# An encoder block on one NeuronCore: memory values copied out of PSUM while their scale is unknown, the first operand in one transfer, eleven unit products at the front

## The chip, the cores and the metric

The kernel runs on one core of one Trainium2 chip. The metric is the device time of one execution in microseconds (us). Before the change the median of three runs is 1365.81 us (1365.35 to 1368.44).

## The reference

One layer of a bidirectional encoder on 256 tokens of width 2048, with 256 memory tokens. All data is float32.

```python
h = rms_norm(x, g_mix);  proj = h @ w_in        # q/k/v of mixers A and B, q of C, three gates
mkv = rms_norm(mem, g_mem[layer]) @ w_mem_kv[layer]
kc = rms_norm(split_heads(mkv[..., :C_W], C_HEADS), g_kc[layer])
vc = split_heads(mkv[..., C_W:], C_HEADS)
...
x = x + merged @ w_o[layer]
hf = rms_norm(x, g_ffn[layer]) @ w_ffn_in[layer]
x = x + (jax.nn.silu(hf[..., :D_FF]) * hf[..., D_FF:]) @ w_ffn_out[layer]
```

Mixer A is a dilated window attention with a relative bias, B a grouped-query attention with rotary embedding, C a cross-attention of four heads into the memory. Their outputs are multiplied by sigmoid gates, merged and projected. For this change two things matter: the memory's normalised rows are projected to four key heads (kc) and four value heads (vc), and a row's normalisation is a single factor per token, so that it can be applied after the projection.

## The kernel before

**Products.** Every float32 operand is split in two parts (`split`, L129): ScalarE writes the rounded high part (whi, or the high half of memT, xT, V: L132 without a scale, L135 with one), VectorE the remainder (wlo: L133, L136). A product of two operands is then three matmuls: high by high, high by low, low by high. All matmuls are issued through one helper line, L79. Weights come in blocks of 512 KB (two k-tiles of 128 rows by 512 columns), loaded by SP into seven raw buffers (`load`, L216), and split into four buffers of whi and four of wlo. A block gives 12 matmuls of 128x512.

**The first stages.** `beginning` (L807) projects the memory through `pair` with two column blocks at once: c = 0 gives the four kc heads in the banks mmY and mmX (tag "at"), c = 1 the four vc heads in mmW and mmQ (tag "tp"; there are two banks of that tag). In this stage the splits of `pair` stand in line 438 (`halves`, whi) and line 448 (`low`, wlo). Then eight calls of `product` (L232) multiply x by w_qkv, one block of 512 columns each; they take their two banks by turns from the tags "c1" and "tp" (made = 1 takes "c1", made = 2 "tp"). Each result goes to `take_slots` (L657) as a job beside the products.

**take_slots.** For heads other than values it copies the bank to SBUF at once, on ScalarE: the squares to sq (L667), the values to y (L668); VectorE sums the squares (L669). Value heads stay in their banks until the rows' scale is known: a job yields as long as its name is not in `known` (L672), and then V is split from the bank, scaled by the row factor (L679, through `split`, L135 and L136), one head and one half of the tokens at a time. The row factor comes from `row_sums` (L288): four row blocks are loaded into SBUF, squared and summed by ScalarE (L296), and a Newton iteration on VectorE (`root_of`, L138) gives the factor. It runs beside the memory projection for the memory ("mem"), and beside the first product for x. Key and query heads are then scaled (L691), multiplied by their gain on GpSimd (L712) and transposed by TensorE (hT).

**Slots.** The tiles rows, y, sq, oneh, row and others are allocated by `s4` and share five slots of 4 KB per partition (pool mid, L111).

**What sets the order.** Inside `run` (the memory projection, and everything from the merging on) TensorE's and SP's instructions keep the program's order. In the products over w_qkv and the attention beside them, the order on each engine is computed from priorities and simulated times when the kernel is built; jobs advance by one step at each k-tile (`tick`, L189), and what stands in a high_priority block goes first. Each engine then executes its instructions in that order.

**The first microseconds.** After the identity matrix is there, TensorE runs unit products on it (L349 to L351). The first operand block (memT, k = 0 and 1) is loaded in two halves of 128 KB with the two halves of the first weight block between them: `whole` (L499) calls `operand(0, True, 1)`, then `load` with two parts, and `load` calls `between` ahead of its second part.

Of the kernel before, what the change touches and what calls it, by code (L numbers as in the profile page):

```python
# [14 lines left out]
AF = mybir.ActivationFunctionType  # L15
# [3 lines left out]
P = 128  # L19
S = 256  # L20
T = S // P
D = 2048
KT = D // P
HD = 128
# [3 lines left out]
PK = 2  # L28
# [75 lines left out]
def encoder_block(ctx: ExitStack, tc: tile.TileContext, a: dict, out: bass.AP):  # L104
    nc = InOrder(tc)
# [16 lines left out]
    def s4(shape, name, dt=F32):  # L122
        return mid.tile(shape, dt, name=name, tag="s4")
# [89 lines left out]

        free.append(place_of.pop(id(raw))[1])

    def load(src, k0, nk, parts=1, between=None):  # L216

        place = free.pop(0)
        raw = place[0].tile([P, PK, NC], F32, name=place[1], bufs=1)
        place_of[id(raw)] = raw, place  # L220
        c = k0 % PK * NC
        for k in range(0, nk, nk // parts):
            n = nk // parts
            if k and between:
                between(k0 + k)
            nc.sync.dma_start(out=raw[:, k:k + n].rearrange("p k n -> p (k n)"),
                              in_=src[k0 // PK][:, c + k * NC:c + (k + n) * NC])
        return raw
# [32 lines left out]
    def load_T(src, g, tag):  # L261


        tiles = [s8([P, 4, 2, S], tag) for _ in range(KT // 4)]
        raws, fetched, have = {}, set(), set()

        def get(k, fetch=False, n=2):
            k0 = k // 2 * 2
            tl = tiles[k // 4]
            ks = range(k0, k0 + 2) if n == 2 else (k,)  # L270
            if k0 not in raws:
                raws[k0] = early.tile([P, 2, S], F32, name="rawT", bufs=4)
            if not fetched.intersection(ks):
                nc.sync.dma_start(out=raws[k0][:, ks[0] - k0:ks[0] - k0 + n],
                                  in_=src[k0 // 2].rearrange("p (k s) -> p k s", s=S)[:, ks[0] - k0:ks[0] - k0 + n])
            fetched.update(ks)
            if not fetch:
                for i in ks:
                    if i not in have:
                        have.add(i)  # L280
                        split(tl[:, i % 4, 0], tl[:, i % 4, 1], raws[k0][:, i - k0], g[:, i:i + 1])
            return tl[:, k % 4, 0], tl[:, k % 4, 1]
        get.tiles = tiles
        return get

    known = set()
# [60 lines left out]
    make_identity(tc.nc, ident)  # L347

    idle = bank("idle", "tp")  # L349
    for _ in range(8):  # L350
        nc.tensor.matmul(idle[:, :P], lhsT=ident, rhs=ident, start=True, stop=True)  # L351

    two = const.tile([P, 2], F32, name="two")
# [96 lines left out]
    def pair(src, lhs, lists, done, doubles=(), forms=None, operand=None, fresh="", early=False, by_halves=False):  # L450
# [48 lines left out]
        def whole(u, c):  # L499
            def ready():  # L500
                last_kind[0] = ""
                parts = 2 if operand and u + c == 0 else 1
                if operand and c == 0:
                    operand(2 * u, True, 3 - parts)
                raw = load((src(u, c),), 0, PK, parts, lambda k: operand(k, True, 1))
                if parts == 2:
                    pass
                elif operand and c == 0:
                    operand(2 * u)
                elif operand and 2 * u + 2 < KT:  # L510
                    operand(2 * u + 2, True)
                hi, lo = halves(*(raw[:, k] for k in range(PK)) if parts == 2 else (raw,),
                                each=(lambda k: operand(k, False, 1)) if parts == 2 else None)
                release(raw)

                def products():
                    halved = by_halves and c == 0 and left[ends[0][1]] == 2
                    for i in range(2 * T):
                        t, k = (i % T, i // T) if parts == 2 else (i // 2, i % 2)
                        st = at(2 * u + k, t)  # L520
                        if not (halved and t):
                            mul(ends[c][t], st, hi[:, k], lo[:, k], parts == 2)
                    for i in range(4 * halved):
                        st, k = at(2 * u + i % 2, 1), i % 2
                        mul(ends[0][1], st, hi[:, k], lo[:, k], cols=slice(i // 2 * NC // 2, (i // 2 + 1) * NC // 2))
                    ending()
                return products
            return ready
# [128 lines left out]
    def take_slots(ps, slots, r, name="x"):  # L657

        n = sum(s[0][0] != "v" for s in slots)
        if n:  # L660
            y = s4([P, T, 4, HD], "y")
            sq = s4([P, T, 4, HD], "sq")
            ss = small.tile([P, T, 4], F32, name="hss")
            with tc.high_priority():
                for t in range(T):
                    src = ps[t][:, :n * HD].rearrange("p (n d) -> p n d", d=HD)
                    nc.scalar.activation(sq[:, t, :n], src, AF.Square)  # L667
                    nc.scalar.activation(y[:, t, :n], src, AF.Copy)  # L668
                nc.vector.tensor_reduce(ss[:, :, :n], sq[:, :, :n], axis=AX.X, op=ALU.add)  # L669
        if name not in known:  # L670
            yield EVAC_LAG
        while name not in known:  # L672
            yield None
        with tc.high_priority():
            for i in range(n, len(slots)):
                v = s2.tile([P, 2, T, HD], F32R, name="V", tag="s2")
                V[slots[i]] = v
                for t in range(T):
                    split(v[:, 0, t], v[:, 1, t], ps[t][:, i * HD:(i + 1) * HD], r[:, 0, t:t + 1])  # L679
        if n:  # L680
            yield EVAC_LAG
            v = small.tile([P, T, 4], F32, name="hv")
            f = small.tile([P, T, 4], F32, name="hf")
            each = lambda w: r[:, w].unsqueeze(2).broadcast_to([P, T, n])
            nc.vector.tensor_mul(ss[:, :, :n], ss[:, :, :n], each(1))
            nc.vector.tensor_scalar(v[:, :, :n], ss[:, :, :n], 1.0 / HD, EPS, op0=ALU.mult, op1=ALU.add)
            nc.vector.tensor_mul(f[:, :, :n], rsqrt(v[:, :, :n], [P, T, n]), each(0))
            yield EVAC_LAG
            for t in range(T):
                for j in range(n):  # L690
                    nc.scalar.activation(y[:, t, j], y[:, t, j], AF.Copy, scale=f[:, t, j:j + 1])  # L691
            turned = slots[0][0][1] == "b"
            rot = s4([P, T, 4, HD], "rot") if turned else None
            j = 0
            while j < n:
                m = 1
                while j + m < n and slots[j + m][0] == slots[j][0]:
                    m += 1
                if turned:
                    tab = turns[:, ("qb", "kb").index(slots[j][0])]  # L700
                    for t in range(T):
                        cs, sn = (tab[:, w, t].unsqueeze(1).broadcast_to([P, m, HD]) for w in range(2))
                        yt, other = y[:, t, j:j + m], sq[:, t, j:j + m]
                        nc.vector.tensor_mul(rot[:, t, j:j + m], yt, cs)
                        pairs = lambda v: v.rearrange("p n (d c) -> p n d c", c=2)
                        for c in range(2):
                            nc.vector.tensor_mul(pairs(other)[:, :, :, c], pairs(yt)[:, :, :, 1 - c],
                                                 pairs(sn)[:, :, :, c])
                        nc.vector.tensor_add(rot[:, t, j:j + m], rot[:, t, j:j + m], other)
                else:  # L710
                    g = gh[:, HEAD_GAINS.index(slots[j][0])]
                    nc.gpsimd.tensor_mul(y[:, :, j:j + m], y[:, :, j:j + m],  # L712
                                         g.unsqueeze(1).unsqueeze(1).broadcast_to([P, T, m, HD]))
                j += m
            y = rot if turned else y
        if n:
            yield HEAD_LAG
            for j in range(n):
                tp = bank("hT")
                for t in range(T):  # L720
                    nc.tensor.transpose(tp[:, t * P:(t + 1) * P], y[:, t, j], ident)
                hT = s2.tile([P, 2, S], F32R, name="headT", tag="s2")
                with tc.high_priority():
                    split(hT[:, 0], hT[:, 1], tp[:, :S])
                headT[slots[j]] = hT
                if j % 2 and j < n - 1:
                    yield 1
        yield 2
        run_jobs()
# [374 lines left out]
```

## Time and profile before

| | |
|---|---|
| median of 3 runs | 1365.81 us |
| lowest, highest | 1365.35, 1368.44 us |
| profiled execution | 1366.78 us, its span 1365.0 us |
| granted TensorE clock, mean of the span | 0.997 |
| TensorE, VectorE, ScalarE busy | 99%, 85%, 63% |
| read from HBM | 297.17 MB, 220 GB/s over the span |

The span runs from the first to the last instruction of the profiled execution. A row of the timeline gives the start in us from the start of the span, the duration, the engine, the line, the operation, what it writes and reads, and how many instructions were merged into it; in brackets stand the engine's idle time before it and what ended it. A row of busy time in a stretch gives for the stretch its length and the busy time of TensorE's matmuls (PE), its weight loads (PEld), VectorE (DVE), ScalarE (ACT) and GpSimd (POOL), each with its number of instructions, then the granted TensorE clock as a share of full speed, the DMA engines' busy share and GB/s. SPq rows are DMA issues of SyncE.

### The profile page before, as it was taken

What the parts mean: (1) busy time and instruction counts of PE and PEld (TensorE: products, weight loads), DVE (VectorE), ACT (ScalarE), POOL (GpSimd) and SP (SyncE); (2) the same over time, 40 slices, a digit from 0 to 9 for tenths busy, and PEclk for the clock granted to TensorE, in tenths of its full rate; (3) what the DMA queues carried; (4) which work ended last, traced back from release to release, by engine and by line L of the source; (5) the groups of instructions that cost most, each with busy time, mean ns of one, the idle gap of its engine ahead of it and who ended that gap; (6) DMA issues with size and microseconds to landing.
All of it is one profiled execution on the core that took longest, in us unless ns stands there. A gap on an engine that the chain in (4) does not pass through costs nothing.

```text
span 1365.0 us, 17319 instructions
## 1 busy us (share of the span) xinstructions
PE 1354.4 (99%) x6170; PEld 1122.6 (82%) x6170; DVE 1157.6 (85%) x1412; ACT 855.6 (63%) x1110; POOL 53.1 (4%) x60
## 2 busy tenths in 40 slices
PE   9989999999999999999999999999999999999998
PEld 7878888888888888888888888888888888888887
DVE  6768876778879779878899998888999889989997
ACT  7766656556656565656776666555666655566664
POOL 0010001000000000000000000000000000000000
PEclk9989999999999999999999999999999999999999
DMA  9967555546785594785578666787666786666873
GB/s 358 351 186 220 155 153 171 171 132 212 256 289 190 183 312 141 264 286 148 191 232 270 187 213 212 244 262 234 202 227 203 249 272 191 227 219 213 278 220 103
DMA packets 86486, 301.18 MB, mean 221 GB/s; under 512 B 9792, under 2 KB 12608, under 8 KB 86144
## 3 DMA queue, kind: packets, MB, share of 16 engines
q1 hardware_dynamic: 79632, 275.94, 58.2%
q0 software_dynamic: 6624, 24.12, 9.4%
q8 instruction: 48, 0.79, 0.2%
q14 instruction: 38, 0.31, 0.1%
q10 hardware_dynamic: 144, 0.02, 0.0%
HBM read 297.17 MB, written 2.88 MB: 220 GB/s over the span
## 4 chain that ended last, share of the span: by engine, by line
PE 94%; DVE 3%; DMA 1%; ACT 1%; issue 1%; SPq 0%; DVEq 0%; ACTq 0%
PE mmX L79 28%; PE mmW L79 19%; PE mm L79 16%; PE mmY L79 15%; PE mmQ L79 11%; DVE wlo L448 2%; PE tp L79 1%; PE sc L79 1%; PE o L79 1%; DMA raw<-in_w_br 1%; ACT whi L438 1%; PE pT L79 1%; PE hT L79 0%; DMA raw<-in_w_mem 0%; DVE raw L583 0%
## 5 line engine op out<-in xcount | busy, mean ns | idle before, releaser
L438 ACT ACTIVATE whi<-raw 128x1024 fp32r<-128x1024 f32 (+1 forms) x363 | 376.9, 1055 | 231.3 <-PE mmQ L79 52.3
L448 DVE TENSOR_TENSOR wlo<-raw,whi 128x1024 fp32r<-128x1024 f32 (+1 forms) x363 | 437.9, 1220 | 84.6 <-ACT whi L438 81.0
L79 PE MATMUL mm<-whi,xT 128*128 128x512 f32 x640 | 205.3, 396 | 3.9 <-DVE V L136 3.9
L79 PEld LDWEIGHTS mm<-whi,xT 128*128 128x128 f32 x640 | 120.6, 190 | 29.3 <-DVE V L136 4.4
L438 ACT ACTIVATE whi<-both 128x1024 fp32r<-128x1024 f32 x101 | 106.5, 1055 | 58.6 <-DVE both L583 18.1
L133 DVE TENSOR_TENSOR wlo<-raw,whi 128x1024 fp32r<-128x1024 f32 x82 | 103.1, 1261 | 42.1 <-ACT whi L132 41.7
L448 DVE TENSOR_TENSOR wlo<-both,whi 128x1024 fp32r<-128x1024 f32 x101 | 123.1, 1222 | 11.6 <-ACT whi L438 10.8
L448 DVE TENSOR_TENSOR wlo<-more,whi 128x1024 fp32r<-128x1024 f32 x89 | 108.7, 1223 | 24.0 <-ACT whi L438 23.0
L438 ACT ACTIVATE whi<-more 128x1024 fp32r<-128x1024 f32 x89 | 93.9, 1058 | 54.2 <-PE mmQ L79 15.4
L79 PE MATMUL mm<-wlo,xT 128*128 128x512 f32 x320 | 126.5, 395 | 0.0
L132 ACT ACTIVATE whi<-raw 128x1024 fp32r<-128x1024 f32 x82 | 86.6, 1061 | 60.4 <-PE mm L79 43.5
L79 PE MATMUL mmW<-whi,forms 128*128 128x512 f32 x368 | 122.1, 391 | 0.0
L79 PE MATMUL mmX<-whi,forms 128*128 128x512 f32 x368 | 122.1, 391 | 0.0
L79 PE MATMUL mmX<-whi,x1T 128*128 128x512 f32 x352 | 120.9, 389 | 0.0
L79 PE MATMUL mmY<-whi,x1T 128*128 128x512 f32 x264 | 89.1, 389 | 0.0
L79 PEld LDWEIGHTS mmW<-whi,forms 128*128 128x128 f32 x368 | 69.1, 188 | 14.2
L79 PEld LDWEIGHTS mmX<-whi,forms 128*128 128x128 f32 x368 | 69.1, 188 | 14.2
L79 PEld LDWEIGHTS mmX<-whi,x1T 128*128 128x128 f32 x352 | 66.1, 188 | 13.7
L79 PE MATMUL mmX<-wlo,forms 128*128 128x512 f32 x184 | 71.7, 389 | 0.0
L79 PE MATMUL mmW<-wlo,forms 128*128 128x512 f32 x184 | 71.7, 389 | 0.0
L79 PEld LDWEIGHTS mm<-wlo,xT 128*128 128x128 f32 x320 | 60.8, 190 | 11.7
L79 PE MATMUL mmX<-wlo,x1T 128*128 128x512 f32 x176 | 68.5, 389 | 0.0
(277 smaller groups left out, 2592.9 us busy)
## 6 DMA issues: line engine op xcount, KB each, us to landing
raw<-in_w_ffn SPq DMA_DIRECT2D x116, 512.0 KB, 5.9
raw<-in_w_gate SPq DMA_DIRECT2D x66, 512.0 KB, 5.0
raw<-in_w_qkv SPq DMA_DIRECT2D x64, 512.0 KB, 4.2
raw<-in_w_ffn_out SPq DMA_DIRECT2D x54, 512.0 KB, 7.1
both<-in_w_ffn SPq DMA_DIRECT2D x33, 512.0 KB, 8.1
more<-in_w_ffn SPq DMA_DIRECT2D x27, 512.0 KB, 6.5
raw<-in_w_o SPq DMA_DIRECT2D x22, 512.0 KB, 4.9
both<-in_w_ffn_out SPq DMA_DIRECT2D x20, 512.0 KB, 5.3
```

The costliest lines, as they stand in the source:

```text
L79: ins = op(*args, **kw)
L132: nc.scalar.activation(hi, src, AF.Copy)
L133: nc.vector.tensor_sub(lo, src, hi.bitcast(F32))
L438: nc.follow(nc.scalar.activation(hi[:, o], v, AF.Copy))
L448: nc.follow(nc.vector.tensor_sub(*due.pop(0)))
```

## The change

Three edits. `take_slots` copies value heads out of their banks to an s4 tile, vraw, with one ScalarE activation per half of the tokens, when the scale of their rows is not known as the kernel is written down; V is then split from vraw. This holds for the memory's four value heads alone; the value heads of x find the scale of x known. The first operand block is loaded by one DMA of 256 KB ahead of both halves of the first weight block, and `between` goes. The unit products at the front are eleven instead of eight.

```diff
-    def load(src, k0, nk, parts=1, between=None):
+    def load(src, k0, nk, parts=1):
...
-            if k and between:
-                between(k0 + k)
...
-        raws, fetched, have = {}, set(), set()
+        raws, have = {}, set()
...
                 raws[k0] = early.tile([P, 2, S], F32, name="rawT", bufs=4)
-            if not fetched.intersection(ks):
-                nc.sync.dma_start(out=raws[k0][:, ks[0] - k0:ks[0] - k0 + n],
-                                  in_=src[k0 // 2].rearrange("p (k s) -> p k s", s=S)[:, ks[0] - k0:ks[0] - k0 + n])
-            fetched.update(ks)
+                nc.sync.dma_start(out=raws[k0], in_=src[k0 // 2].rearrange("p (k s) -> p k s", s=S))
...
-    for _ in range(8):
+    for _ in range(11):
         nc.tensor.matmul(idle[:, :P], lhsT=ident, rhs=ident, start=True, stop=True)
...
-                    operand(2 * u, True, 3 - parts)
-                raw = load((src(u, c),), 0, PK, parts, lambda k: operand(k, True, 1))
+                    operand(2 * u, True)
+                raw = load((src(u, c),), 0, PK, parts)
...
+        held = [ps[t][:, n * HD:].rearrange("p (n d) -> p n d", d=HD) for t in range(T)]
+        if n < len(slots) and name not in known:
+            raw = s4([P, T, 4, HD], "vraw")
+            with tc.high_priority():
+                for t in range(T):
+                    nc.scalar.activation(raw[:, t, n:], held[t], AF.Copy)
+            held = [raw[:, t, n:] for t in range(T)]
         if name not in known:
             yield EVAC_LAG
...
-                    split(v[:, 0, t], v[:, 1, t], ps[t][:, i * HD:(i + 1) * HD], r[:, 0, t:t + 1])
+                    split(v[:, 0, t], v[:, 1, t], held[t][:, i - n], r[:, 0, t:t + 1])
```

## The prediction

> **What bounds the kernel now.** I read the page first, then the chain of waits, then the engines one by one around the one place where the chain leaves TensorE, and the first microseconds. The page:
>
> ```profile
> span 1365.0 us, 17319 instructions
> PE 1354.4 (99%) x6170; PEld 1122.6 (82%) x6170; DVE 1157.6 (85%) x1412; ACT 855.6 (63%) x1110; POOL 53.1 (4%) x60
> PE 94%; DVE 3%; DMA 1%; ACT 1%; issue 1%; SPq 0%; DVEq 0%; ACTq 0%
> ```
>
> TensorE is busy in all but 10.6 us of the span and the chain runs over it for 94%. So only what stops TensorE, or slows its clock, has a price. The chain that ended last, in order of time (start, us, what):
>
> ```profile
> 2.59 5.79 DMA raw<-in_w_mem
> 8.41 1.07 ACT whi L438
> 9.50 1.24 DVE wlo L448
> 10.78 1.42 PE mmW L79 x5
> ...
> 51.67 21.09 PE mm L79 x93
> ...
> 75.82 1.22 DVE wlo L133
> 77.04 0.27 DVE V L136
> ...
> 77.36 9.03 PE mm L79 x28
> 86.39 0.88 PE hT L79 x8
> ```
>
> Up to 10.78 us the chain waits for the second weight block and its split. From there TensorE is continuous to the end of the memory projection (51.67) and through the first 93 matmuls of the first product over w_qkv, 21.09 / 93 = 0.2268 us each. Then the chain leaves it until 77.36. TensorE's rows there (start, us, count, and in brackets the idle time before and what ended it), and after them the engines' busy time in three stretches:
>
> ```profile
> 73.04 0.39 PE L79 MATMUL mm<-whi,xT 128*128 128x512 f32 x1
> 77.36 0.79 PE L79 MATMUL mm<-whi,xT 128*128 128x512 f32 x1 [3.93 <-DVE V L136]
> 82.22 0.76 PE L79 MATMUL mm<-whi,xT 128*128 128x512 f32 x2
> ```
>
> ```profile
> 73.30:77.30 4.00, 0.12 (x1) 0.00 (x0) 3.52 (x9) 4.00 (x11) 0.00 (x0) 0.80 1.02 337
> 77.30:82.30 5.00, 4.94 (x12) 3.88 (x13) 0.93 (x6) 4.12 (x10) 2.38 (x1) 0.50 0.63 188
> 82.30:86.30 4.00, 4.00 (x19) 3.28 (x18) 1.45 (x9) 0.56 (x1) 0.00 (x0) 0.97 0.02 4
> ```
>
> The second product writes the two "tp" banks. They hold the memory values, and those are split out of them by L135 and L136 only when their scale is known:
>
> ```profile
> L135 ACT ACTIVATE V<-mmW,scales x4: 348/348/390, 66.3 to 75.7; 128x128 fp32r<-128x128 f32 x4
> L136 DVE SCALAR_TENSOR_TENSOR V<-mmQ,scales,V x4: 341/342/343, 67.9 to 77.2; 128x128 fp32r<-128x128 f32 x4
> ```
>
> The last split ends at 77.2 + 0.34 = 77.5 (the chain has it end at 77.31), and the matmul at 77.36 follows it.
>
> **The wait that is removed.** The last matmul of the first product starts at 73.04, so the next could start at 73.04 + 0.23 = 73.27. It starts at 77.36: 4.09 us lost. The pause also costs clock. The seventh column of the stretches after the length is the granted clock: 0.80 on average in the pause, 0.50 for the next five us, 0.97 after. From 77.36 to 82.22 TensorE runs 11 matmuls (12 counted in the second stretch, the last of which lies on its edge); at 0.2268 they take 2.49, they took 4.86: 2.37 lost, and about 0.15 more in the two that follow while the clock comes back. Together 2.5 us. With ScalarE's copies the banks come free without the scale. The first of the two copies can start when the last mmQ ends at 51.67. A copy of a whole bank has its price in the same shape on ScalarE, 0.60 here:
>
> ```profile
> 51.70 1.06 ACT L132 ACTIVATE whi<-raw 128x1024 fp32r<-128x1024 f32 x1 [0.28 <-PE mmQ L79]
> 54.42 1.06 ACT L132 ACTIVATE whi<-raw 128x1024 fp32r<-128x1024 f32 x1 [0.86 <-PE mm L79]
> 72.78 0.60 ACT L667 ACTIVATE sq<-mm 128x512 f32<-128x512 f32 x1 [0.42 <-PE mm L79]
> ```
>
> Two of them are 1.2 us of ScalarE. Queued behind them are the whi at 51.70 and two xT splits. That whi fills the last of four buffers and feeds the fourth weight pair of the product (12 matmuls, 2.72 us a pair), due at 51.67 + 8.16 = 59.8; it would be ready by 54. The next whi waits for TensorE anyway. So the copies cost nothing, and they have from 51.67 to 73.27 to be done: even if the vraw tile has to wait for a slot, 21 us of cover is gone before TensorE sees it. The eight splits of V then read SBUF and stay as many; nothing on TensorE waits for them before the attention over the memory.
>
> The Trainium skill ("TensorE: Matmul & The Clock Gate", Part 1) gives the clock as half until a free-running window of about 3.4 us was busy, and half again after an idle one. The rows agree in kind: (0.20 x 4 + 0.50 x 5 + 0.03 x 4) / 0.50 = 6.8 us at half clock, two such windows; by one window alone the clock term would be 1.7 us instead of 2.5 and the sum below 0.8 higher, an estimate from that page.
>
> **What is late next.** With the wait gone TensorE meets ScalarE's and VectorE's work of this stretch 6.6 us earlier than now. These rows set when that work is done today:
>
> ```profile
> 76.15 2.46 ACT L691 ACTIVATE y<-y,hf 128x128 f32<-128x128 f32 x8
> 80.33 1.06 ACT L296 ACTIVATE rows<-rows 128x1024 f32<-128x1024 f32 x1
> 85.74 1.06 ACT L132 ACTIVATE whi<-raw 128x1024 fp32r<-128x1024 f32 x1 [4.26 <-PE mm L79]
> ```
>
> ```profile
> 78.69 2.38 POOL L712 TENSOR_TENSOR y<-y,gh 128x1024 f32<-128x1024 f32 x1 [77.38 <-ACT y L691]
> ```
>
> ```profile
> 81.51 0.16 DVE L298 TENSOR_REDUCE ss<-rss 128x2 f32<-128x4 f32 x1 [3.95 <-ACT rows L296]
> 83.88 0.16 DVE L150 SCALAR_TENSOR_TENSOR rs_y<-rs_t,rs_y 128x2 f32<-128x2 f32 x1
> 86.83 1.23 DVE L133 TENSOR_TENSOR wlo<-raw,whi 128x1024 fp32r<-128x1024 f32 x1 [2.79 <-ACT whi L132]
> ```
>
> Two things can be late. First, the kc transposes (hT, at 86.39 in the chain, after 28 matmuls of the second product). In the same place of the order they would be due at 73.27 + 28 x 0.2268 = 79.6, and GpSimd has their input ready at 78.69 + 2.38 = 81.07: up to 1.45 us. Second, the fifth weight pair. Its whi and wlo wait for TensorE today (4.26 and 2.79 of idle time). Due at 73.27 + 4 x 2.72 = 84.15, its whi can begin behind the last rows at 81.5 and is in time; its wlo stands in VectorE's order behind the chain of x's row scale, which ends at 84.04, and would end at 85.27 against 84.38: 0.9 us. If the first is paid, the second is covered by it. Against both: outside the stages written out by hand, the order of the engines is computed, and as the second product begins earlier in that computation too, the transposes should stand behind more of its matmuls. Bounds 0 and 1.45; I take 0.5, nearer to nothing, since TensorE shows no other wait from here to the end of the attention (its idle time is the front, this pause and the end).
>
> **The front.** The rows of TensorE are the eight unit products, the first real matmul, two late ones of the first weight block and the wait at the second; between them stand two rows of SP's issues:
>
> ```profile
> 1.36 3.78 PE L79 MATMUL idle<-ident 128*128 128x128 f32 x16 [1.36 <-POOL ident masks.py:199]
> 4.79 0.77 PE L79 MATMUL mmY<-whi,memT 128*128 128x512 f32 x1
> ...
> 8.33 0.63 PE L79 MATMUL mmX<-whi,memT 128*128 128x512 f32 x2
> ...
> 8.80 0.40 PE L79 MATMUL mmX<-wlo,memT 128*128 128x512 f32 x1
> ```
>
> ```profile
> 1.65 0.42 SPq L79 DMA_DIRECT2D rawT<-in_memT  x1
> 2.12 0.91 SPq L79 DMA_DIRECT2D raw<-in_w_mem  x2
> ```
>
> ```profile
> 10.78 0.49 PE L79 MATMUL mmW<-wlo,memT 128*128 128x512 f32 x1 [0.76 <-DVE wlo L448]
> ```
>
> Eight products are 16 instructions, (4.79 - 1.36) / 16 = 0.214 us each. Three more are six, 1.29 us: the first real matmul starts near 6.08. What hides it is the wait for the second block, whose wlo is there only at 10.74. The first block's 12 matmuls take 2.72 us at full clock and 12 x 0.427 = 5.1 at the half-clock spacing of the second product, so they end between 8.8 and 11.2. Today the last of them lie (8.80 - 8.33) / 2 = 0.235 apart, so the clock is up by then, and TensorE is busy without a break for longer in the new order: I expect an end near 9.4 and no cost; at the worst it is 0.65 us. The single transfer takes one DMA issue away: 2.12 - 1.65 = 0.47 us, by which the second block's transfer, the head of the chain above, can start earlier. The bytes ahead of it stay the same. If the DMA engines set its landing, nothing is gained; if SP's queue does, 0.47. I take 0.2 gained. The first half block may land later than now, behind the larger operand; it has the same cover as the unit products.
>
> **The sum.** Against the profiled execution, 1366.78 us for a span of 1365.0: 1366.78 - 4.09 - 2.5 - 0.2 + 0.5 = 1360.5. The median of the three runs, 1365.81, lies 0.97 below it. If the profiled execution is longer for a reason outside the pause, the median goes to 1359.5; if it lost more clock in the pause than they did, to 1360.5. I take 1360.0 between them.
>
> **Rivals.** One, the clock part is not in the runs that are timed. For it: three runs spread over 3.1 us (1365.35 to 1368.44), as much as the clock term. Against it: the pause is the same in each, and the profile shows it. Then the gain is 4.09 + 0.2 - 0.5 = 3.8, and 1365.81 goes to 1362.0. By the free-running window of the Trainium skill's page on the clock gate, how long the half clock lasts may differ from one execution to the next; no run here shows its start.
>
> Two, the new tile takes a slot that the fourth load of x's rows needs. The s4 tiles share five slots. After 72.8 us they are kc's y, a row block, the one-hot table, and the sq and y of the first product, and SP's fourth row load indeed goes out as VectorE's sum over sq ends:
>
> ```profile
> 74.39 1.22 DVE L669 TENSOR_REDUCE hss<-sq 128x8 f32<-128x1024 f32 x1 [0.21 <-ACT sq L667]
> 75.64 0.33 SPq L79 DMA_DIRECT2D rows<-in_x  x1
> ```
>
> If vraw is held until 77.5, as V's banks are now, the load is 77.5 - 75.61 = 1.9 later, the row scale with it, and the fifth pair's wlo is 0.9 + 1.9 = 2.8 late instead of the 0.5 taken above: 1362.3. Against it: the eight ScalarE splits stand from 66.3 to 75.7 because each pair waits for VectorE's reads of the same banks; out of SBUF they can go back to back, 8 x 0.35 = 2.8 us from 66.3, and vraw is free near 71. The Trainium skill ("PSUM — Partial Sum Buffer", Terms) says that reads of one bank by ScalarE and VectorE at once are an error, so they must be kept apart; the spacing of these rows agrees.
>
> Three, slower: the same shortage, but it falls on the y of the first product's evacuation, and the slot it gets is that of kc's y, which is free only after the kc transposes. ScalarE, in order, then stands from 73.3 until about 80 (y x8, GpSimd's 2.38, the transposes), the fourth pair's wlo is ready at 84.3 instead of 81.4, the fourth row load, its landing, its square and the scale follow some 8 us late, the fifth wlo is about 8 us late in all, and the clock falls again for 2.5: 10.5 us against the 6.8 gained, 1370. It decides from the point where V's splits end after 73.3 and the slot order is this one. For it: the slots are full to the last. Against: V's scale is there at 66.
>
> Four, the change does not do it: TensorE's matmul at 77.36 waits for something else that V's split only happens to precede, as the wlo that ends at 77.04. Then 1365.8. Against it: the wait names V, and the whi of the second product's first pair, the fifth after that of 51.70, was written long before:
>
> ```profile
> 65.30 1.06 ACT L132 ACTIVATE whi<-raw 128x1024 fp32r<-128x1024 f32 x1 [0.49 <-PE mm L79]
> ```
>
> **How the numbers follow.** Forecast 0.72; clock not in the runs 0.08; row load late 0.11; no gain 0.05; slower 0.04. A measurement of this kernel can tell about 0.2%, 2.7 us, from no change, so faster begins under 1363.1: 0.72 + 0.08 + 0.09, with 0.02 of the row load's chance beyond it, is 0.89; within 0.2% 0.07; slower 0.04. The range: 1365.81 - 4.09 - 2.5 - 0.47 = 1358.75 with every term at its best, less 0.45 for the scatter of a median; up to 1362.6, which takes in the clock and the row load.
>
> **What would show it.** TensorE goes from the last matmul of the first product to the next without idle time, the groups that wait for V are gone, the granted clock is 1.00 from 73 to 87; two 128x512 copies of ScalarE lie near 52; V's splits read vraw and end by about 71; 22 unit matmuls end near 6.1 and mmW's wlo still starts between 10.3 and 10.8. I am wrong in the middle if TensorE shows idle time of over a microsecond before hT or at the fifth pair, in the slots if ScalarE's sq and y of the first product lie far apart, in the front if mmW starts after 10.8.

## The result and the profile after

| | before | after |
|---|---|---|
| median, us | 1366.16 (6 runs) | 1359.78 (6 runs) |
| lowest, highest, us | 1365.35, 1368.44 | 1359.53, 1360.31 |
| profiled execution, us | 1366.78 | 1359.78 |
| mean granted clock of the profiled execution | 0.997 | 1.000 |

The changed kernel is faster: the ratio of the times is 0.9951, with a 95% interval of 0.9939 to 0.9964, or 6.4 us between the medians. Between the two profiled executions it is 7.0 us. In the times of the changed kernel two things stand out at once: they are lower, and they lie within 0.8 us of each other where those of before lie within 3.1. Both come back below. Neither number is fixed: measured once more (the last experiment), the changed kernel was 8.7 us below before, and its five times lay within 2.2 us.

The page of the changed kernel, with the same lines as before (span; busy time of each engine; shares of the chain of waits):

```profile
span 1358.0 us, 17334 instructions
PE 1351.8 (100%) x6176; PEld 1121.4 (83%) x6176; DVE 1157.1 (85%) x1412; ACT 856.4 (63%) x1112; POOL 53.1 (4%) x60
PE 94%; DVE 3%; DMA 1%; issue 1%; ACT 1%; SPq 0%; DVEq 0%; ACTq 0%
```

TensorE was busy in all but 10.6 us of the span before and is in all but 6.2 now, 4.4 us less. The span is 7.0 us shorter. The other 2.6 us are TensorE's own work going faster, with six instructions more: that is the clock behind the pause. (In the front the further units take 1.3 us and the products behind them about as much less: up to the same product, at 12.0 and 11.27, TensorE is busy for 9.6 and 9.5 us.)

The chain that ended last, in order of time (start, us, what):

```profile
2.12 5.53 DMA raw<-in_w_mem
...
10.05 1.45 PE mmW L79 x5
...
50.96 33.55 PE mm L79 x148
84.51 0.87 PE hT L79 x8
```

Before, the chain left TensorE after 93 matmuls and came back at 77.36 through V's last split. Now one piece of 148 matmuls runs from the first product into the second: 96 are the first product, 52 the second, and only then come the transposes of kc. The front has moved as well: the second weight block's transfer starts at 2.12 instead of 2.59 and takes 5.53 instead of 5.79, and mmW's wlo product starts at 10.05 instead of 10.78.

Busy time by engine in three stretches laid as before around the seam of the two products (length; PE, PEld, DVE, ACT, POOL each with its count; granted clock; DMA share; GB/s):

```profile
72.60:76.60 4.00, 4.00 (x19) 3.34 (x18) 3.19 (x7) 4.00 (x11) 0.00 (x0) 1.00 1.01 351
76.60:81.60 5.00, 5.00 (x23) 4.13 (x23) 3.22 (x2) 5.00 (x9) 2.41 (x1) 1.00 0.69 226
81.60:85.60 4.00, 4.00 (x23) 3.41 (x22) 3.33 (x9) 3.14 (x8) 0.00 (x0) 1.00 0.80 248
```

PE is full in all three and the clock is 1.00 where it was 0.80, 0.50 and 0.97. The copies and the splits that follow them, on ScalarE's timeline and in the groups of the tile V (the last by count, then min/median/max ns, then first and last start):

```profile
50.23 0.61 ACT L670 ACTIVATE vraw<-mmW 128x512 f32<-128x512 f32 x1
51.50 0.61 ACT L670 ACTIVATE vraw<-mmQ 128x512 f32<-128x512 f32 x1
```

```profile
L135 ACT ACTIVATE V<-vraw,scales x8: 384/386/390, 65.6 to 67.6; 128x128 fp32r<-128x128 f32 x8
L136 DVE SCALAR_TENSOR_TENSOR V<-vraw,scales,V x8: 345/348/353, 66.9 to 68.8; 128x128 fp32r<-128x128 f32 x8
```

The banks are empty at 52.1, 20.6 us before the second product wants them. The splits start when the scale is there, as they did, but stand back to back: VectorE's last one ends at 69.2 instead of 77.5.

### The profile page after: what moved, and what is told of

Its sections match the earlier page's. It is cut to its first block, busy times and chain, and to the rows that moved or that the text cites. A ratio compares the mean times of both kernels' runs of the same rounds, so it can differ in the third digit from the quotient of the medians.

```text
span 1358.0 us, 17334 instructions
## 1 busy us (share of the span) xinstructions
PE 1351.8 (100%) x6176; PEld 1121.4 (83%) x6176; DVE 1157.1 (85%) x1412; ACT 856.4 (63%) x1112; POOL 53.1 (4%) x60
## 4 chain that ended last, share of the span: by engine, by line
PE 94%; DVE 3%; DMA 1%; issue 1%; ACT 1%; SPq 0%; DVEq 0%; ACTq 0%
PE mmX L79 28%; PE mmW L79 20%; PE mm L79 16%; PE mmY L79 15%; PE mmQ L79 11%; DVE wlo L443 2%; PE tp L79 1%; PE sc L79 1%; PE o L79 1%; DMA raw<-in_w_br 1%; ACT whi L433 1%; PE pT L79 1%; PE hT L79 0%; DMA raw<-in_w_mem 0%; DVE raw L578 0%
## 5 line engine op out<-in xcount | busy, mean ns | idle before, releaser
L79 PE MATMUL mm<-whi,xT 128*128 128x512 f32 x640 | 202.3, 393 | 0.0
```

Source lines behind the costliest of these rows:

```text
L79: ins = op(*args, **kw)
```

## The experiments

Each kernel was measured beside the kernel before on the same chip. "Ratio" is its time over that of before, with the 95% interval.

### Each half of the change alone

**The copies alone**: the kernel before with only the take_slots edit, so with the old front.

```diff
...
+            raw = s4([P, T, 4, HD], "vraw")
...
+                    nc.scalar.activation(raw[:, t, n:], held[t], AF.Copy)
...
-                    split(v[:, 0, t], v[:, 1, t], ps[t][:, i * HD:(i + 1) * HD], r[:, 0, t:t + 1])
+                    split(v[:, 0, t], v[:, 1, t], held[t][:, i - n], r[:, 0, t:t + 1])
```

> The kernel before with ScalarE's two copies alone; the operand stays in two transfers and there are eight unit products. By my account the pause and its clock loss go (4.09 + 2.5) and the front stays: first product follows the memory projection at 51.67 and the second follows the first at 73.3 without a break, mmW's first wlo matmul at 10.78 as before, granted clock 1.00, 1366.2 - 6.0 to 6.6 = 1359.6 to 1360.2, some 0.5 us above the changed kernel. If the front carried a large part of the gain (rival), the time stays above 1361.5.

Measured: 1360.34 us (1360.09 to 1362.66), ratio 0.9954 [0.9941, 0.9968]. The pause is gone; the chain runs through the seam in one piece:

```profile
53.99 37.63 PE mm L79 x166
```

That piece starts at 53.99 where 51.67 was expected. The profiled run is the slowest of its five, 1362.66, and its trace shows why, in the front (the chain's transfer of the second block, then two stretches):

```profile
2.60 6.57 DMA raw<-in_w_mem
```

```profile
8.00:11.50 3.50, 1.72 (x6) 0.86 (x5) 1.23 (x2) 2.20 (x4) 0.00 (x0) 1.00 1.04 413
11.50:15.00 3.50, 3.44 (x8) 2.77 (x9) 3.44 (x6) 3.09 (x5) 0.00 (x0) 0.51 1.03 407
```

The block landed at 9.17, TensorE was busy for 49% of the first stretch, and in the next it ran at half clock: 8 matmuls in 3.5 us. That is a second clock loss, in a place where the prediction had looked for none.

**The front alone**: the changed kernel without the copies, V split from the banks as before.

```diff
-                    split(v[:, 0, t], v[:, 1, t], held[t][:, i - n], r[:, 0, t:t + 1])
+                    split(v[:, 0, t], v[:, 1, t], ps[t][:, i * HD:(i + 1) * HD], r[:, 0, t:t + 1])
```

> The changed kernel without the copies: V is split out of the banks as before, the front is the new one. By my account the pause of 3.9 us in front of the second product is there again, with the half clock behind it; only the front's 0.73 us is left: mmW's first wlo matmul at 10.05, 1366.2 - 0.7 = 1365.5. If the copies are not the cause, it is near 1360.

Measured: 1360.03 us (1359.65 to 1360.39), ratio 0.9952 [0.9939, 0.9964]. The expectation failed: without a single copy the pause is gone as well. V is still split from mmW and mmQ, in four pairs, one weight block apart. Two rows of ScalarE's timeline in the kernel before, and then three of the front alone, show what differs:

```profile
74.71 1.08 ACT L132 ACTIVATE whi<-raw 128x1024 fp32r<-128x1024 f32 x1
75.65 0.39 ACT L135 ACTIVATE V<-mmW,scales 128x128 fp32r<-128x128 f32 x1
```

```profile
63.73 0.37 ACT L135 ACTIVATE V<-mmW,scales 128x128 fp32r<-128x128 f32 x1
...
71.53 0.35 ACT L135 ACTIVATE V<-mmW,scales 128x128 fp32r<-128x128 f32 x1
...
72.56 0.60 ACT L662 ACTIVATE sq<-mm 128x512 f32<-128x512 f32 x1 [0.42 <-PE mm L79]
```

In the kernel before, ScalarE's order was: third pair of V, then sq, y, sq, y of the first product (the sq at 72.78 that the prediction quotes), a whi, and only then the fourth pair. Each sq needs the last matmuls that write its bank, the second one the very last of the first product, so the fourth pair, which the next matmul waits for, could not start before TensorE had run dry. With the new front the order computed for ScalarE is one weight block earlier for V: the first pair is at 63.73 instead of 66.27 and the fourth, at 71.53, stands ahead of that sq. The sq is not the whole of it, though. VectorE was still reading the banks for the third pair until 73.71 (first row), and where nothing else stood between two pairs, in the kernel held at 12 without copies (below), ScalarE waited for VectorE's reads of the pair before (second row):

```profile
73.37 0.34 DVE L136 SCALAR_TENSOR_TENSOR V<-mmQ,scales,V 128x128 fp32r<-128x128 f32 x1
```

```profile
83.95 0.37 ACT L135 ACTIVATE V<-mmW,scales 128x128 fp32r<-128x128 f32 x1 [2.23 <-DVE V L136]
```

So in the kernel before the fourth pair would have been somewhat late even without the sq; by how much, no run shows. How close the front alone comes to the pause shows in its chain:

```profile
72.97 0.27 DVE V L136
...
73.28 11.63 PE mm L79 x50
```

The chain has the last split end at 73.24, and the product goes on at 73.28. There is no margin, and the chain still runs over V.

### Is it V, and do the copies free TensorE from the scale?

If that reading is right, a scale that comes later brings the pause back in the front alone and not in the changed kernel. `hold(n, ...)` in `beginning` sets by how many steps the memory's row sums are put off; before and after it is 6.

**Held 8, no copies** (the front alone, with this edit):

```diff
-        start(hold(6, row_sums(a["mem"], r_m, 3, "mem")))
+        start(hold(8, row_sums(a["mem"], r_m, 3, "mem")))
```

> The kernel with the new front alone (no copies) and the memory's row sums started two k-tiles later (hold 8 for 6). The new front alone measured 1360.03, against what I had forecast; in its ScalarE order all four pairs of V's splits stand ahead of the squares of the first product, in the order before the fourth pair stands behind them. By this new account a later scale puts the fourth pair behind them again and the pause of about 4 us with its half clock returns: 1360.0 + 4 to 6.6 = 1364 to 1366.6. By the rival, that the new front itself removes the pause, 1360.0 within 0.5.

Measured: 1365.48 us (1364.57 to 1366.59), ratio 0.9986 [0.9977, 0.9995]. TensorE's row after the pause, and two stretches:

```profile
76.09 0.80 PE L79 MATMUL mm<-whi,xT 128*128 128x512 f32 x1 [3.94 <-DVE V L136]
```

```profile
74.00:78.00 4.00, 1.91 (x5) 1.52 (x6) 2.09 (x4) 4.00 (x12) 0.57 (x1) 0.52 0.63 181
78.00:82.00 4.00, 4.00 (x13) 3.15 (x12) 3.17 (x13) 0.90 (x3) 1.80 (x1) 0.62 0.18 73
```

Two steps of a job far ahead of it bring the whole pause back: 3.94 us of idle time, then half clock. ScalarE's order is again the one of before: the third pair of V at 70.44, the first sq at 71.52, the fourth pair at 74.39.

**Held 12, no copies**, and **held 12 with the copies** (the changed kernel with the same edit):

> As the one before, with the row sums six k-tiles later (hold 12). V's last two pairs then stand behind the scaling of the kc heads too. By my account the pause in front of the second product grows to 8 to 11 us and the time to 1370 to 1374; by the rival 1360.

> The changed kernel, copies included, with the row sums six k-tiles later (hold 12). V's splits come as late as in the kernel beside it, but the banks were emptied near 52 us: no pause in front of the second product, 1359.8 within 1. If the copies do nothing for the pause (rival), 1370 or more, as without them.

Measured: 1374.64 us (1374.32 to 1375.61), ratio 1.0054 [1.0040, 1.0068] without the copies; 1359.90 us (1359.07 to 1360.72), ratio 0.9947 [0.9932, 0.9962] with them. The pause without the copies is somewhat longer than the 8 to 11 us expected. TensorE's row after the pause without the copies, then, of the kernel with them, V's splits on VectorE and the chain over the seam:

```profile
84.84 0.79 PE L79 MATMUL mm<-whi,xT 128*128 128x512 f32 x1 [12.72 <-DVE V L136]
```

```profile
L136 DVE SCALAR_TENSOR_TENSOR V<-vraw,scales,V x8: 345/346/348, 76.2 to 78.2; 128x128 fp32r<-128x128 f32 x8
```

```profile
50.53 44.21 PE mm L79 x195
```

With the copies V is split as late as 78.5, and TensorE goes on from 50.53 to 94.74 without a wait. The same late scale costs 14.7 us without them. This is what the copies do, and in this pair it is shown apart from the order.

**The scale early, no copies, old front**: the kernel before with `hold(2, row_sums(..., 2, "mem"))` in place of `hold(6, row_sums(..., 3, "mem"))`.

> The kernel before with the memory's row sums started after two k-tiles instead of six, and two apart instead of three; no copies, old front. If it is the lateness of the scale in ScalarE's order that makes the pause, the pause goes without any copy, V's last split being in time before 73 us: 1366.4 - 6.0 = 1360.4 within 0.7, with some runs 2 us higher, as in the other kernels with the old front. If the banks are held by something other than the scale (rival), 1366.

Measured: 1360.59 us (1359.28 to 1363.43), ratio 0.9950 [0.9938, 0.9963]. V's last split starts at 63.5, and the pause is gone:

```profile
L136 DVE SCALAR_TENSOR_TENSOR V<-mmQ,scales,V x4: 344/344/345, 53.7 to 63.5; 128x128 fp32r<-128x128 f32 x4
```

So there are three ways out of the same pause, each worth 6.1 to 7.4 us by itself against before on the same chip (6.06, 7.39 and 6.37): empty the banks early, bring the scale early, or let the computed order fall so that the fourth pair stands ahead of the sq.

### Is the clock behind the pause real time?

**The pause filled**: the kernel before, with seventeen more products of 128x512 in the gap between the first and the second product. They work on xT, write a bank of their own, and nothing reads them. They and the last matmuls of the first product are kept in the program's order, so that they lie in the gap; the rest is as before.

```diff
...
+        if made[0] == 1:
...
+            for _ in range(17):
+                nc.tensor.matmul(fill, lhsT=xT.tiles[3][:, 3, 0, :P], rhs=rows, start=True, stop=True)
```

> The kernel before with 17 idle matmuls of 128x512 between the last matmul of the first product and the first of the second (17 x 0.2268 = 3.86 us, the length of the pause); their results are not used. The banks come free no earlier, but TensorE does not stand still. By my account the pause stays and the clock loss goes: the second product starts at 77.4 as before, its matmuls are 0.227 apart from the first one on, granted clock 1.00, 1366.2 - 2.0 to 2.5 = 1363.7 to 1364.2, and the runs spread less than the 3.1 us of the kernel before. By the rival, that the clock loss is not in the timed runs, 1366.2.

Measured: 1364.92 us (1363.69 to 1367.10), ratio 0.9990 [0.9981, 0.9998]. The rows of TensorE at the seam, and the stretch behind it (the profiled run, 1367.05, fell to half clock in the front like that of the copies alone, so all of it lies some 2.7 us later than in the profile of before):

```profile
75.92 4.01 PE L79 MATMUL fill<-xT 128*128 128x512 f32 x17
80.02 0.50 PE L79 MATMUL mm<-whi,xT 128*128 128x512 f32 x1
```

```profile
80.00:82.00 2.00, 1.98 (x9) 1.64 (x10) 0.22 (x1) 2.00 (x6) 0.65 (x1) 1.00 0.74 231
```

The product still has to wait for V (the chain has V's last split end at 79.97), but it goes on at full clock. Useless work made the kernel faster, by 1.5 us between the medians; by the interval the gain may be anything from 0.3 to 2.6 us. The runs were expected to spread over less than 3.1 us; they spread over 3.4, and those of before beside them over 4.0. How much the clock is worth is best read among runs that lost no clock elsewhere: of the runs of before beside it, nine have a mean granted clock of 0.999 (median 1366.22); of the filled kernel, nine have 0.999 or 1.000 (median 1364.46). That is 1.8 us, less than the 2.5 of the profiled execution, whose mean clock is 0.997. The kernel held at 8 points the same way: its seven runs at 0.999 have a median of 1365.07, its four at 0.997 one of 1366.09. The loss behind the pause seems to come in two sizes, about 1 us apart.

### The front

**Eight units**: the changed kernel with the old number of unit products. **The operand in two transfers**: the changed kernel with the old loading, so copies and eleven units.

```diff
-    for _ in range(11):
+    for _ in range(8):
```

> The changed kernel with eight unit products instead of eleven. By my account the three more unit products are idle work under the wait for the second weight block: mmW's first wlo matmul stays at 10.05 within 0.1 and the time at 1359.8 within 0.3. By the rival, that they bring TensorE's clock up in time, the first block ends later than 9.3 us, mmW's wlo starts after 10.3 and the time is 0.3 us or more above 1359.8.

```diff
...
-                    operand(2 * u, True)
-                raw = load((src(u, c),), 0, PK, parts)
+                    operand(2 * u, True, 3 - parts)
+                raw = load((src(u, c),), 0, PK, parts, lambda k: operand(k, True, 1))
...
```

> The changed kernel with the first operand in two transfers again (copies and eleven unit products stay). The profile of the copies alone has the clock at half from 11.7 to 15 us, behind waits of 0.7, 1.1 and 0.8 us of the first blocks, and 2.3 us more on the clock at the first product. If TensorE's waits among the first blocks do that, then three more unit products fill the first of them and no run of this kernel has it: 1360.0 within 0.5 and runs within 1 us of each other. If the single transfer is what keeps the clock, some runs lie 2 us and more above the fastest, as with the copies alone (1360.09 to 1362.66).

Measured: eight units 1359.14 us (1359.01 to 1361.27), ratio 0.9950 [0.9938, 0.9963], which can't be told from the changed kernel; its mmW wlo product lies at 10.25, between the two forecasts, so the trace does not decide between them either. Two transfers 1360.77 us (1359.32 to 1362.26), ratio 0.9951 [0.9938, 0.9963], and the profiled run, 1362.26, again ran into half clock, though eleven units ran ahead of it. I had taken the units for what keeps the clock; that fell. Its transfer of the second block and two stretches:

```profile
2.60 6.27 DMA raw<-in_w_mem
```

```profile
8.20:11.60 3.40, 1.36 (x5) 0.61 (x4) 1.62 (x3) 2.61 (x4) 0.00 (x0) 0.93 1.03 401
11.60:15.00 3.40, 3.40 (x10) 2.64 (x10) 3.34 (x6) 3.01 (x5) 0.00 (x0) 0.56 1.03 412
```

The same two stretches of the kernel before and of the changed one, in which the clock stayed:

```profile
8.20:11.60 3.40, 2.32 (x9) 1.34 (x9) 2.10 (x4) 2.92 (x4) 0.00 (x0) 1.00 1.02 412
11.60:15.00 3.40, 3.40 (x16) 2.80 (x15) 3.33 (x5) 2.94 (x5) 0.00 (x0) 1.00 1.04 408
```

```profile
8.20:11.60 3.40, 3.02 (x14) 2.17 (x13) 2.83 (x4) 3.10 (x5) 0.00 (x0) 1.00 1.04 419
```

Where TensorE was busy 2.32 or 3.02 of the 3.4 us (68%, 89%) the clock stayed; with 1.36 (40%) it fell. This goes with the landing of the second block. With the operand in two transfers it landed at 8.38, 8.42, 8.87, 9.17 and 9.59 in the five profiles that show it, and the clock fell in the last three; with one transfer it landed at 7.09 to 8.14 in six, and the clock fell in none. Over all runs without the pause, or with it filled, 5 of 26 with two transfers have a mean clock of 0.998, and none of 35 with one. So the single transfer is worth two things: some half a microsecond in most executions (the copies alone have a median of 1360.3 in their four runs at 0.999 or 1.000, the changed kernel 1359.8, though not beside it), and the half clock that now and then cost 2 us more (1362.66 in the fifth). The kernel before can have that loss besides the one behind the pause, in its two sizes; this is a likely reason for its scatter of 3 us, though only the profiled runs show where their clock fell, and it is not the only one: the changed kernel, measured again below, scatters by 2.2 us with a mean clock of 1.000 in each run.

**The second block in halves** too: the changed kernel with the second weight block loaded and split in two parts like the first, so that its products can start on the first half; then the same with eight units; and beside them the changed kernel once more.

```diff
-                parts = 2 if operand and u + c == 0 else 1
+                parts = 2 if operand and u == 0 else 1
...
```

> The changed kernel with the second weight block loaded and split in two halves as well, so that mmW's low parts need not wait for the split of the whole block: the wait of 0.38 us at mmW and what lies around it goes, one more DMA issue of 0.47 us stands ahead of the later blocks. By my account mmW's products follow the first block at 9.3 without idle time: 0.3 to 0.6 us faster than the changed kernel beside it. By the rival, that the later blocks then come too late, no gain or a loss of up to 0.5.

> As the one before, with eight unit products. The first block can then start near 5.2 instead of 6.1 us. With the second block in halves the wait behind it is gone, so a start 0.9 us earlier counts up to the landing of the second block: 0 to 0.5 us faster than the one before. If the three unit products keep the clock up, some runs lie 2 us above the fastest.

> The changed kernel once more, beside the next three on the same chip: 1359.8 within 0.5, the second weight block landed between 7.0 and 8.2 us, granted clock 1.00 from 8 to 15 us.

Measured on one chip: the changed kernel again 1359.30 us (1358.80 to 1361.00), ratio 0.9940 [0.9928, 0.9953]; in halves 1359.05 us (1358.35 to 1359.83), ratio 0.9936 [0.9924, 0.9949]; in halves with eight units 1358.22 us (1357.99 to 1359.36), ratio 0.9931 [0.9917, 0.9944]. In that last kernel the first real product starts at 5.20, mmW follows at 8.61 without a wait, and the only wait of the front is 0.16 us:

```profile
5.20 1.22 PE L79 MATMUL mmY<-whi,memT 128*128 128x512 f32 x2
...
8.61 0.62 PE L79 MATMUL mmW<-whi,memT 128*128 128x512 f32 x2
...
11.90 0.50 PE L79 MATMUL mmY<-wlo,memT 128*128 128x512 f32 x1 [0.16 <-DVE wlo L443]
```

It is the lowest of all, 1.1 us below the changed kernel on the same chip by the medians, though the two intervals overlap. The halves by themselves gave 0.25 us, less than the 0.3 to 0.6 expected and within the scatter; leaving the three units out gave another 0.8, more than the 0 to 0.5 expected. It fits that once the second block no longer holds TensorE up, three more units only delay the first product. So does the second profile of the changed kernel: there the second block was in early, TensorE has no wait in the front at all, and the chain goes back to the units:

```profile
1.37 5.06 PE idle L79 x22
```

## Why the prediction was right, and where it was not

**The pause, -4.09.** It went in full: the last matmul of the first product is followed by the next with no idle time. Both copies took 0.61 us (0.60 was taken from the row of sq), began at 50.23 and 51.50, and made TensorE wait for nothing. V's splits ended at 69.2, near the 71 that was named. Rivals two and three fell with that: SP's fourth load of x's rows went out at 74.93, 0.71 earlier than before, and ScalarE's sq and y of the first product followed each other from 72.08 to 74.14.

```profile
74.93 0.33 SPq L79 DMA_DIRECT2D rows<-in_x  x1
```

Rival four fell by the kernels held at 8 and 12: the later V is split, the longer the wait, and with the copies there is none.

What the prediction had wrong here is the cause behind the cause. It said why TensorE waited (V's banks) and never asked why V's fourth pair came as late as 75.65 when its scale was there at 66. A part of the answer stood in its own rows: sq at 72.78, waiting for TensorE, ahead of V on the same engine. (What it said of the pairs, that each waits for VectorE's reads of the pair before, is borne out by the row at 83.95 above.) Had it been asked, it would have been seen that a shift of the computed order can remove the pause, and that the two halves of the change overlap: 6.1 us for the copies alone, 6.4 for the front alone, 6.4 for both. So the time of the changed kernel does not show what the copies do; it is 1359.78 with them and 1360.03 without. The pair held at 12 shows it. That the front counts for a few tenths holds only with the copies in place.

**The clock, -2.5.** It is real time, and rival one is out: filling the pause without shortening it gained 1.5 us between the medians, and 1.8 among the runs that lost no clock elsewhere. But 2.5 is the size of the profiled execution, where half clock held for twice 3.41 us; the middle run lost about 1.8. The prediction allowed for that when it set the median between 1359.5 and 1360.5. The runs bear out the rule that it quoted of the Trainium skill ("TensorE: Matmul & The Clock Gate", Part 1), a free-running window, as far as they go: the same pause seems to cost one kernel two different amounts. By the same page one window would have been 1.7, an estimate. The prediction says that no run shows where the half clock starts; the trace does, and the last section reads it.

**The front, -0.2.** This term was mis-sized. Its bounds were 0 and 0.47; the profiles show 10.78 - 10.05 = 0.73, of which 2.59 - 2.12 = 0.47 is the issue and 0.26 the faster landing. That is one pair of profiles: in all of them mmW's wlo product came between 9.43 and 10.53 with one transfer and between 10.78 and 11.98 with two. "The bytes ahead of it stay the same" was right and did not settle it. What was missed altogether is that the front has a clock loss of its own. The units did as forecast in this profile: the first real product starts at 6.08, and the wait for the second block hides the delay:

```profile
1.36 5.07 PE L79 MATMUL idle<-ident 128*128 128x128 f32 x22 [1.36 <-POOL ident masks.py:199]
6.08 1.09 PE L79 MATMUL mmY<-whi,memT 128*128 128x512 f32 x2
...
9.06 0.39 PE L79 MATMUL mmX<-wlo,memT 128*128 128x512 f32 x1
...
10.05 0.50 PE L79 MATMUL mmW<-wlo,memT 128*128 128x512 f32 x1 [0.38 <-DVE wlo L443]
```

The first block's matmuls end at 9.45 (9.4 was expected), and of the 0.76 us wait 0.38 is left.

**Lateness, +0.5.** It was nothing. GpSimd had the transposes' input ready at 79.89, and the transposes came at 84.51, because the computed order had put 52 matmuls of the second product ahead of them instead of 28. The doubt was stated in the prediction, which took 0.5 all the same.

```profile
77.48 2.41 POOL L714 TENSOR_TENSOR y<-y,gh 128x1024 f32<-128x1024 f32 x1 [76.17 <-ACT y L693]
```

**The sum.** -6.3 was forecast against the profiled execution and -7.0 measured; the front gave 0.5 more, the lateness 0.5 that was not paid, and 0.3 goes the other way. Most of that is lost later: at the start of a piece of 84 matmuls in the chain the changed kernel is 298.81 - 291.42 = 7.39 ahead, as much as 4.09 + 2.5 + 0.73 make, and behind a load of w_br near 340 (10.64 us before, 10.85 after) 384.69 - 377.50 = 7.19. For the median, 4.09 + 1.8 + 0.5 for the front make the 6.4 that was measured, but the 0.5 is itself read off the runs. Two terms missed in the same direction and one, the clock, in the other. That 1360.0 came out within 0.2 us of the measured 1359.78 is therefore in part luck; the pause, the largest term, was not.

**What stays open.** Why the second block lands later when the operand comes in two transfers: their number and the length of their rows were changed together. Why the eight-unit kernel has two runs above 1360.6 among three near 1359.1, and the changed kernel, measured again, one of 1361.00, all at a mean clock of 0.999 or 1.000.

## What to carry to other kernels

Ask of a wait not only what it waits for but what stands ahead of that on its own engine: here the split that TensorE waited for stood behind an instruction that waited for TensorE. Where the order is computed, a small edit far away can close or open such a loop, so test each edit alone, and test the robust fix (here, a copy that needs nothing late) by making its input late on purpose. The scatter of a kernel's times, with the granted clock of each run beside it, can point to a loss that its one profiled execution happens not to have.

## What the runs showed of the hardware

The granted clock fell without any long wait. In the front of the kernel with two transfers and eleven units TensorE's only waits over half a microsecond around the fall were these two:

```profile
10.00 0.50 PE L79 MATMUL mmW<-whi,memT 128*128 128x512 f32 x1 [1.28 <-ACT whi L438]
11.26 0.80 PE L79 MATMUL mmW<-wlo,memT 128*128 128x512 f32 x1 [0.76 <-DVE wlo L448]
```

The Trainium skill ("TensorE: Matmul & The Clock Gate", Why this matters for your kernels) warns of idle gaps above about 3 us. Here gaps of 1.28 and 0.76 us, in a stretch that was busy for 40% of 3.4 us, were enough; 49% in the kernel with the copies alone was too little as well, and 68% in the kernel before was enough to keep the clock.

The moments at which the clock changed can be read from short stretches. In the kernel before it fell at 75.69, while TensorE stood, and rose at 82.52:

```profile
75.60:75.69 0.09, 0.00 (x0) 0.00 (x0) 0.01 (x1) 0.09 (x2) 0.00 (x0) 1.00 1.40 341
75.70:75.80 0.10, 0.00 (x0) 0.00 (x0) 0.00 (x0) 0.10 (x2) 0.00 (x0) 0.50 0.84 184
82.40:82.50 0.10, 0.10 (x2) 0.10 (x1) 0.07 (x1) 0.00 (x0) 0.00 (x0) 0.50 0.00 0
82.53:82.60 0.07, 0.07 (x2) 0.02 (x2) 0.07 (x1) 0.00 (x0) 0.00 (x0) 1.00 0.00 0
```

Half clock held for 6.83 us there and in the kernel held at 8, for 13.65 in the one held at 12 without copies, and for 3.41 in the three fronts where it fell (the copies alone, the filled pause, two transfers with eleven units): one, two or four times 3.41 us. In the 3.41 us up to each of these six falls TensorE was busy for at most 47%. In the 3.41 us behind the falls in the fronts it was busy for 93% or more, and the clock came back at their end; behind the falls in the pauses of before and of held 8 it was busy for 1.74 and 1.50 us of them, and half clock held for as long again. So where these steps of 3.41 us lie against a wait seems to set whether the wait costs none, one or two of them. That this is what sets the runs of one kernel apart is not shown: in no profile did half clock behind the pause hold for one step.
